# First feed-forward of a decoder trunk: the fifth quad's weight forms join the written-out order, and squares, norm, gates and first down chunk come later

## The chip, the core and the metric

The kernel runs as one program on one core of a Trainium2 chip. The metric is the device time of one execution in microseconds (us); smaller is better. A core has several engines that work side by side, each through a queue of its own that is taken strictly in the order in which the program lists it: PE (matrix products), DVE (elementwise), ACT (elementwise with tables, copies), POOL, and SP, which here only issues transfers. An instruction waits for other engines by semaphores, and what stands behind it on its engine waits with it.

## The reference

A trunk of two layers on a sequence of 512 positions and width 1024. Each layer adds half of a gated feed-forward, a mixer with three head groups, and half of a second feed-forward. What is touched here is the very first feed-forward:

```
def _rmsnorm(x, g):
    y = xf * lax.rsqrt(jnp.mean(xf * xf, axis=-1, keepdims=True) + EPS)
    return (y * g.astype(jnp.float32)).astype(x.dtype)

def _swiglu(x, w_gate, w_up, w_down):
    return (jax.nn.silu(x @ w_gate) * (x @ w_up)) @ w_down

x = x + MACARON * _swiglu(_rmsnorm(x, ffn1_norm), ffn1_w_gate, ffn1_w_up, ffn1_w_down)
```

The width of the hidden layer is 2816; all is float32.

## The kernel before

Activations lie transposed: 1024 features in four pairs of 128-row blocks (`x0` to `x3`), 512 positions along a row. Each float32 operand of a product is split into a high part (a rounded copy that ACT makes, L89) and a low part (the difference, which DVE makes, L90); one product is then three matmuls, high by high, high by low, low by high. Function `parts` (L87) issues the two halves of such a split.

The columns of the gate and up weights are taken in 22 quads of 256 columns by 512 positions, gates and ups in turn. A quad isn't multiplied in the plain way but by seven products of half size (a Strassen-like scheme), each of 12 matmuls of 128 rows by 256 columns. Products 1, 2 and 3 use three weight blocks directly (tile `wd`), products 6 and 7 use sums of blocks (tile `wa`), products 4 and 5 others (tile `wb`). Function `forms_steps` (L132) gives the steps that build them: `direct` makes `wd`, `first` adds two blocks (L148) and makes `wa`, `second` adds two (L154) and makes `wb`. Tiles `wa` and `wb` come from one pool tag with three buffers (`w2`). The result of a product is fetched from the accumulator by ACT or DVE in `after` (L349 to L366): product 1 is copied by L353, 2 added by L355, 6 copied by L357, 5 by L359, 7 subtracted at L361, 3 at L363, 4 copied by L365. Products 1, 6, 7 and 4 of a quad share one accumulator (`pa`), so PE can't start product 6 before ACT has copied product 1 away.

The norm isn't applied to `x` ahead of the products. Products take the raw `x` with its gain, and the reciprocal root of the mean square is multiplied in when a gate is finished. So the squares (L237 on ACT, the sums L240 and L243 on DVE), the column sums (`norm_columns`: four small matmuls L250, then L252 and a power on POOL, L254) and the row form (`norm_rows`: L264, four matmuls L265, copy L267) may come late, but before the first `done` (L368), which multiplies a gate by that row, applies Silu on ACT, multiplies again, and later multiplies the up half by the gate and splits the result into tile `h`.

The first two quads are multiplied in the plain way in function `start` (L419), while `x` and weights arrive. There, within `tc.manual_schedule`, the instructions of DVE and ACT stand in the order in which the code lists them; everything else is ordered by the scheduler from priorities and buffer counts. Quads 2 and 3 have their forms in the set order; quad 4 (whose weights lie in separate tiles, `rawa`) has its own made later, by `begin` (L329). A list of products, in `gate_up` (L308), says when each product and each block of the down projection (`schedule`, L502) is to come; function `start` returns a list of calls made after the products, one each: the tenth is `norm_columns`, the twelfth `norm_rows` with the two first `done`. The tag `u` has two buffers, which the up results and the tiles of squares share.

Of the kernel before, what the change touches and what calls it, by code (L numbers as in the profile page):

```python
# [9 lines left out]
F32 = mybir.dt.float32  # L10
F32R = mybir.dt.float32r
AF = mybir.ActivationFunctionType
ALU = mybir.AluOpType
AX = mybir.AxisListType

P = 128
D = 1024
T = 512
# [9 lines left out]
KP = KT // 2  # L28
# [20 lines left out]
def trunk(ctx, tc, xt, w_first, w_gu1, w_dn1, w_in, w_out, w_gu2, w_dn2, w_last, par, con, wst, bst, gvr, gain, out):  # L49
    nc = tc.nc  # L50
# [2 lines left out]
    wpool = ctx.enter_context(tc.tile_pool(name="wpool", bufs=1))  # L53
    spool = ctx.enter_context(tc.tile_pool(name="spool", bufs=2))
    pp = ctx.enter_context(tc.tile_pool(name="pp", bufs=8, space=bass.MemoryType.PSUM))
    stage = {}

    def bank(name):
        return pp.tile([P, T], F32, tag="ps", name=name)
# [6 lines left out]
    def uniq(s):  # L66
        uid[0] += 1
        return f"{s}{uid[0]}"
# [18 lines left out]
    def parts(hi, lo, src):  # L87

        nc.scalar.copy(hi, src)  # L89
        nc.vector.tensor_tensor(lo, src, hi.bitcast(F32), ALU.subtract)  # L90

    def load(src):
        n = src.shape[-1] * (src.shape[1] if len(src.shape) == 3 else 1)
# [79 lines left out]
    split = parts  # L173


    state = {}
    warm_ps = bank("warm")
    xf = [None] * KP

# [55 lines left out]
    def squares(m):  # L235
        sq = scratch(1, "sq")
        nc.scalar.activation(sq, xp[m], AF.Square)  # L237
        if m == 0:
            state["acc"] = spool.tile([P, T], F32, tag="acc", name=uniq("acc"), bufs=1)
            nc.vector.tensor_tensor(state["acc"], sq[:, :T], sq[:, T:], ALU.add)  # L240
        else:
            for i in range(2):
                nc.vector.tensor_tensor(state["acc"], state["acc"], sq[:, i * T : (i + 1) * T], ALU.add)  # L243
# [64 lines left out]
    def gate_up(w_gu, first, others, tail, from_start=False):  # L308
# [7 lines left out]
        quads = [(p, j) for p in range(FP) for j in range(2)]  # L316
        steps = [(7 * q + t, 0, q, n) for q in range(len(quads)) for n, t in WHEN.items()]
        if from_start:
            moved = {(3, 1): 15.3, (3, 2): 15.6, (2, 4): 27.5}
            steps = [(moved.get((q, n), t), k, q, n) for t, k, q, n in steps]  # L320
        steps += [(t, 1, None, work) for t, work in others]
        steps.sort(key=lambda e: e[:2])
        live, gates, raws = {}, {}, {}
# [25 lines left out]
        def after(q, n):  # L349
            c11, c21, c12, c22 = [quarter(q, i) for i in range(4)]  # L350
            b = live[q]
            if n == 1:
                state["copied"] = nc.scalar.copy(c11, b["pa"])  # L353
            elif n == 2:
                nc.vector.tensor_tensor(c11, b["pb"], c11, ALU.add)  # L355
            elif n == 6:
                state["copied"] = nc.scalar.copy(c12, b["pa"])  # L357
            elif n == 5:
                state["copied"] = nc.scalar.copy(c22, b["pc"])  # L359
            elif n == 7:  # L360
                nc.vector.tensor_tensor(c22, c22, b["pa"], ALU.subtract)  # L361
            elif n == 3:
                nc.vector.tensor_tensor(c12, b["pc"], c12, ALU.subtract)  # L363
            else:
                nc.scalar.copy(c21, b["pa"])  # L365
                done(q)  # L366

        def done(q):  # L368
            p, j = quads[q]
# [18 lines left out]
        else:  # L388
            begin(0)
            begin(1)  # L390
            for m in range(KP):
                for q in (0, 1):
                    for n in (1, 2):
                        ps = psum(q, ("pa", "pb")[n - 1])
                        hi, lo = live[q]["w"][n]
                        bh, bl = form(m, MOVING[n])
                        c = slice(m * P, (m + 1) * P)
# [4 lines left out]
            wait = lambda: None  # L402
# [16 lines left out]
    def start(live, done, ahead, raws_of):  # L419

        for k in range(12):
            warm = warm_ps[:, (k % 4) * P : (k % 4 + 1) * P]
            nc.tensor.matmul(warm, lhsT=ones, rhs=ones, start=True, stop=True)
        pool = stage["pool"]
        extra = pool.tile([P, 4 * T], F32R, tag="hp", name="a21", bufs=4)
        a21 = [(extra[:, m * H : (m + 1) * H], extra[:, (4 + m) * H : (5 + m) * H]) for m in range(KP)]
        raws = [wpool.tile([P, 1024], F32, tag="pt", name=uniq("rawp"), bufs=3) for _ in range(KP - 1)]  # L430
        raws.append(wpool.tile([P, 12 * P], F32, tag="wdn", name=uniq("rawp"), bufs=2)[:, :1024])
        for k in (1, 0):
            nc.sync.dma_start(x[k], xt[:, k, :])
            nc.sync.dma_start(raws[0][:, (1 - k) * T : (2 - k) * T], w_first[0, :, (1 - k) * T : (2 - k) * T])
        for m in range(1, KP):
            nc.sync.dma_start(xp[m], xt[:, 2 * m : 2 * m + 2, :])
            nc.sync.dma_start(raws[m], w_first[m])
        ahead(2)
        ahead(3)
        ahead(4)  # L440
        ws, rooms = [], []
        steps2 = forms_steps(raws_of(2))
        steps3 = None
        with tc.manual_schedule(engines={mybir.EngineType.DVE, mybir.EngineType.Activation}):
            for m in range(KP):
                w = wpool.tile([P, 2048], F32R, tag="w2", name=uniq("wf"), bufs=3)
                ws.append(w)
                if m == 0:
                    parts(w[:, :T], w[:, 1024 : 1024 + T], raws[m][:, :T])
                norm_pair(m, G1, True)  # L450
                gained(m, 0, G1, a21[m][0], a21[m][1], slice(H, T))
                if m == 0:
                    parts(w[:, T:1024], w[:, 1024 + T :], raws[m][:, T:])
                else:
                    parts(w[:, :1024], w[:, 1024:], raws[m])
            for m in range(KP):
                r = pool.tile([P, 4 * T], F32, tag="hp", name=uniq("xw"), bufs=4)
                rooms.append(r)
                sums_of(m, G1, r[:, : 4 * H], r[:, 4 * H : 6 * H])
                if m:  # L460
                    sum_parts(m - 1, rooms[m - 1][:, : 4 * H])
                if m == 1:
                    steps2[1]()
            steps3 = forms_steps(raws_of(3))
            steps3[1]()
            sum_parts(KP - 1, rooms[KP - 1][:, : 4 * H])
            for f in steps2[2:] + steps3[2:]:
                f()
        ahead(5)
        ps = [[bank(uniq("pg")) for _ in range(2)] for _ in range(2)]  # L470
        for m in range(KP):
            kw = {"skip_group_check": True}
            for j in range(2):
                b11, b21, b22, b12 = [
                    [ws[m][:, o + j * T + i * P : o + j * T + (i + 1) * P] for o in (0, 1024)] for i in range(4)
                ]
                hi, lo = xf[m][:, H : 3 * H], xf[m][:, 8 * H : 10 * H]
                for i, w in ((0, b21), (1, b22)):
                    mm3(ps[j][i], w[0], w[1], hi, lo, m == 0, False, **kw)
                for i, w in ((0, b11), (1, b12)):  # L480
                    for t, a in ((slice(0, H), form(m, A11)), (slice(H, T), a21[m])):
                        mm3(ps[j][i][:, t], w[0], w[1], a[0], a[1], False, m == KP - 1, **kw)
        for j in range(2):
            c = pool.tile([P, 2 * T], F32, tag="gu"[j], name=uniq("gu"[j]), bufs=2)
            for i in range(2):
                nc.scalar.copy(c[:, i * T : (i + 1) * T], ps[j][i])
            live[j] = {"c": c}
        for j, w in ((0, steps2[0]), (1, steps3[0])):
            c = pool.tile([P, 2 * T], F32, tag="gu"[j], name=uniq("gu"[j]), bufs=2)
            live[2 + j] = {"w": w, "c": c}  # L490
        for m in range(KP):
            squares(m)

        def rows():
            norm_rows()
            done(0)
            done(1)

        wait = lambda: None
        return [wait] * 9 + [norm_columns, wait, rows]  # L500

    def schedule(l, w_dn, hs):  # L502

        def run(d, p0, p1):
            p = bank(uniq("pdn"))
            block_down(p, l, w_dn, d, 2 * p0, hs[2 * p0 : 2 * p1], True, True)
            add_down(d, p)

        held = {}

        def fetch_first(d):
            with tc.issue_after(state["fetched"].ins):
                held[d] = down_raw(l, w_dn, d, 0, 2 * CHUNKS[0][1])

        def split_first(d):
            with tc.issue_after(state["copied"].ins):
                held[d] = down_parts(held[d], 2 * CHUNKS[0][1])

        def run_first(d):
            p = bank(uniq("pdn"))  # L520
            down_products(p, held.pop(d), hs[: 2 * CHUNKS[0][1]], True, True)
            add_down(d, p)

        jobs = []
        for p0, p1 in CHUNKS[:-1]:
            for d in range(KT):
                t = 14 * p1 + 10 + 3.5 * d
                if p0:
                    jobs.append((t, lambda d=d, p0=p0, p1=p1: run(d, p0, p1)))
                else:  # L530
                    jobs.append((t - 10, lambda d=d: fetch_first(d)))
                    jobs.append((t - 4, lambda d=d: split_first(d)))
                    jobs.append((t, lambda d=d: run_first(d)))
        return jobs

    def ffn(l, w_gu, w_dn, after):
        with tc.tile_pool(name=uniq("ffn"), bufs=1, reuse_waits="tile") as pool:
# [6 lines left out]
                opened[d] = bank(uniq("pdn"))  # L544
                block_down(opened[d], l, w_dn, d, f0, hs[f0:f1], True, False)

            others = schedule(l, w_dn, hs)
            others += [(14 * p1 + t, lambda d=d: open_block(d)) for d, t in enumerate((0, 3, 6, 7))]

            def tail():  # L550
# [407 lines left out]
```

## Time and profile before

| what | us |
|---|---|
| three timed runs | 1816.51, 1817.70, 1818.04 |
| their median | 1817.7 |
| the profiled execution, whole time | 1817.61 |
| its span, first to last instruction | 1815.9 |
| PE busy in the span | 1802.4 (99%) |
| DVE busy | 1326.5 (73%) |
| ACT busy | 826.1 (45%) |
| POOL busy | 121.0 (7%) |

The span is what the trace covers; 1.7 us of the profiled execution lie around it. A busy PE isn't a PE at its peak: matmuls are pipelined, so the distance from start to start counts, not the length of a row. In rows of the timeline the first number is the start, the second the duration; a bracket at the end gives the idle time before the instruction and what ended it.

### The profile page before, as it was taken

How to read it: one execution, taken by the hardware profiler on the slowest of the kernel's cores; microseconds unless marked ns; L12 is line 12 of the kernel's file. 1: busy time of each engine (PE TensorE's matmuls, PEld its weight loads, DVE VectorE, ACT ScalarE, POOL GpSimd, SP SyncE). 2: the span in 40 equal slices, each digit the busy share in tenths (PEclk: the TensorE clock that was granted, in tenths of full speed). 3: DMA queues.
4: the chain of work that ended last, by engine and by line, in shares of the span. 5: the costliest groups of instructions: out<-in, count | busy, mean ns of one | idle time of the engine just before them, and what ended most of it. 6: DMA issues, size and time to landing. Idle time of an engine off the chain costs nothing.

```text
span 1815.9 us, 28447 instructions
## 1 busy us (share of the span) xinstructions
PE 1802.4 (99%) x11576; PEld 1646.1 (91%) x11576; DVE 1326.5 (73%) x1828; ACT 826.1 (45%) x1224; POOL 121.0 (7%) x121
## 2 busy tenths in 40 slices
PE   9999999999999999999999999999999999999998
PEld 8999999888889999999899999998888899999996
DVE  8877777674687877777888777766657788777765
ACT  7544444413345544444554444434133455444443
POOL 1100000000100000000000000000000000000000
PEclk9999999999999999999999999999999999999999
DMA  7665655522223855556457555573322257565632
GB/s 244 164 160 153 153 145 150 176 81 93 70 82 82 223 145 151 150 156 157 128 129 197 148 152 148 152 190 115 98 70 70 70 144 196 151 155 157 157 88 82
DMA packets 120899, 251.19 MB, mean 138 GB/s; under 512 B 10048, under 2 KB 12352, under 8 KB 120512
## 3 DMA queue, kind: packets, MB, share of 16 engines
q1 hardware_dynamic: 97072, 204.02, 35.5%
q0 software_dynamic: 23408, 45.09, 15.3%
q8 instruction: 90, 1.47, 0.3%
q14 instruction: 41, 0.34, 0.1%
q10 hardware_dynamic: 288, 0.27, 0.0%
HBM read 247.25 MB, written 2.10 MB: 137 GB/s over the span
## 4 chain that ended last, share of the span: by engine, by line
PE 94%; DVE 4%; issue 1%; ACT 1%; DMA 0%; POOL 0%; SPq 0%; POOLq 0%; ACTq 0%; DVEq 0%
PE pa L281 9%; PE pa L282 9%; PE pa L283 9%; PE pdn L169 8%; PE pdn L170 8%; PE pdn L171 8%; PE pc L282 4%; PE pc L283 4%; PE pc L281 4%; PE pb L283 2%; PE pb L282 2%; PE pb L281 2%; PE pqk L169 2%; PE pqk L171 2%; PE pqk L170 2%; PE pout L171 2%
## 5 line engine op out<-in xcount | busy, mean ns | idle before, releaser
L169 PE MATMUL pdn<-h,wdn 128*128 128x512 f32 x632 | 247.6, 392 | 0.0
L170 PE MATMUL pdn<-h,wdn 128*128 128x512 f32 x632 | 247.6, 392 | 0.0
L171 PE MATMUL pdn<-h,wdn 128*128 128x512 f32 x632 | 246.0, 389 | 0.3 <-DVE wdn L90 0.3
L89 ACT CAST wd<-rawq 128x1024 fp32r<-128x1024 f32 (+1 forms) x170 | 133.4, 832 | 183.8 <-PE pc L283 170.3
L281 PE MATMUL pa<-xf,wa 128*128 128x256 f32 x688 | 195.7, 284 | 1.5 <-ACT g L353 1.5
L283 PE MATMUL pa<-xf,wa 128*128 128x256 f32 x688 | 195.3, 284 | 0.2 <-DVE wa L90 0.2
L282 PE MATMUL pa<-xf,wa 128*128 128x256 f32 x688 | 195.2, 284 | 0.0
L90 DVE TENSOR_TENSOR wd<-rawq,wd 128x1024 fp32r<-128x1024 f32 (+1 forms) x170 | 155.3, 954 | 48.6 <-ACT wd L89 48.4
L89 ACT CAST wdn<-rawd 128x512 fp32r<-128x512 f32 (+1 forms) x152 | 97.2, 639 | 176.2 <-PE pdn L171 173.5
L112 POOL DMA_DIRECT2D rawq<-in_w_gu x85 | 93.0, 1095 | 1241.7 <-DMA rawq<-in_w_gu 806.1
L89 ACT CAST w<-raw 128x1024 fp32r<-128x1024 f32 x77 | 80.9, 1051 | 205.3 <-PE pqk L171 60.6
L90 DVE TENSOR_TENSOR w<-raw,w 128x1024 fp32r<-128x1024 f32 x77 | 94.1, 1222 | 70.5 <-ACT w L89 69.8
L171 PEld LDWEIGHTS pdn<-h,wdn 128*128 128x128 f32 x632 | 118.7, 188 | 26.4 <-DVE wdn L90 0.7
L169 PEld LDWEIGHTS pdn<-h,wdn 128*128 128x128 f32 x632 | 119.2, 189 | 21.0
L170 PEld LDWEIGHTS pdn<-h,wdn 128*128 128x128 f32 x632 | 119.2, 189 | 19.5
L281 PEld LDWEIGHTS pa<-xf,wa 128*128 128x128 f32 x688 | 132.5, 193 | 2.6 <-ACT g L353 1.7
L283 PEld LDWEIGHTS pa<-xf,wa 128*128 128x128 f32 x688 | 132.6, 193 | 0.5 <-DVE wa L90 0.4
L90 DVE TENSOR_TENSOR wdn<-rawd,wdn 128x512 fp32r<-128x512 f32 (+1 forms) x152 | 107.0, 704 | 35.4 <-ACT wdn L89 35.4
L282 PEld LDWEIGHTS pa<-xf,wa 128*128 128x128 f32 x688 | 132.6, 193 | 0.0
L306 DVE SCALAR_TENSOR_TENSOR x<-pdn,x 128x512 f32<-128x512 f32 x152 | 103.8, 683 | 3.8 <-PE pdn L171 3.8
L90 DVE TENSOR_TENSOR wa<-rawq,wa 128x1024 fp32r<-128x1024 f32 x85 | 103.6, 1219 | 1.9 <-ACT wa L89 1.9
L90 DVE TENSOR_TENSOR wb<-rawq,wb 128x1024 fp32r<-128x1024 f32 x85 | 103.5, 1218 | 0.2 <-ACT wb L89 0.2
(283 smaller groups left out, 5041.1 us busy)
## 6 DMA issues: line engine op xcount, KB each, us to landing
rawq<-in_w_gu SPq DMA_DIRECT2D x170, 512.0 KB, 5.7
rawq<-in_w_gu POOLq DMA_DIRECT2D x85, 512.0 KB, 5.8
rawd<-in_w_dn SPq DMA_DIRECT2D x140, 256.0 KB, 4.5
raw<-in_w_in SPq DMA_DIRECT2D x52, 512.0 KB, 3.5
rawq<-in_w_gu SPq DMA_DIRECT2D x85, 256.0 KB, 6.0
raw<-in_w_out SPq DMA_DIRECT2D x16, 512.0 KB, 3.5
rawd<-in_w_dn SPq DMA_DIRECT2D x12, 384.0 KB, 3.2
raw<-in_w_last SPq DMA_DIRECT2D x6, 512.0 KB, 4.1
```

What stands on the lines that cost most here:

```text
L89: nc.scalar.copy(hi, src)
L90: nc.vector.tensor_tensor(lo, src, hi.bitcast(F32), ALU.subtract)
L112: nc.gpsimd.dma_start(two[:, :, 1, :], src.rearrange("p (n s c) -> p n s c", n=2, s=2)[:, :, 0, :], accum_op=ALU.add)
L169: nc.tensor.matmul(ps, lhsT=ah, rhs=bh, start=first, stop=False, **kw)
L170: nc.tensor.matmul(ps, lhsT=ah, rhs=bl, start=False, stop=False, **kw)
L171: nc.tensor.matmul(ps, lhsT=al, rhs=bh, start=False, stop=last, **kw)
L281: nc.tensor.matmul(ps, lhsT=hi[:, c], rhs=bh, start=one, stop=False, skip_group_check=True)
L282: nc.tensor.matmul(ps, lhsT=hi[:, c], rhs=bl, start=False, stop=False, skip_group_check=True)
L283: nc.tensor.matmul(ps, lhsT=lo[:, c], rhs=bh, start=False, stop=m == pairs[-1], skip_group_check=True)
L306: nc.vector.scalar_tensor_tensor(x[d], p, 0.5, x[d], ALU.mult, ALU.add)
```

## The change

Five edits, all but one within the first feed-forward's start.

- The forms of quad 4 (`steps4`) are built at the end of the set order, after those of quads 2 and 3, not by `begin`.
- The squares of the four pairs are issued behind the last low-part difference that was recorded (`state["split"]`).
- The norm's columns come after the sixteenth product of the list, its rows after the eighteenth, not the tenth and twelfth.
- The four first gates and ups aren't finished as their products end or two at once, but one after each of the next four products (`gates`). The results of the first two quads lie in one tile of tag `hp`.
- Product 4 of quad 2 isn't moved in the list any more, and the first chunk of the down projection is due 7 steps later.

```diff
@@ gate_up @@
-            moved = {(3, 1): 15.3, (3, 2): 15.6, (2, 4): 27.5}
+            moved = {(3, 1): 15.3, (3, 2): 15.6}
@@ after @@
                 nc.scalar.copy(c21, b["pa"])
-                done(q)
+                if not (from_start and q < 4):
+                    done(q)
@@ start @@
-            for f in steps2[2:] + steps3[2:]:
+            steps4 = forms_steps(raws_of(4))
+            for f in steps2[2:] + steps3[2:] + steps4[1:]:
                 f()
...
-            c = pool.tile([P, 2 * T], F32, tag="gu"[j], name=uniq("gu"[j]), bufs=2)
+            if j == 0:
+                c01 = pool.tile([P, 4 * T], F32, tag="hp", name=uniq("c"), bufs=4)
+            c = c01[:, 2 * j * T : 2 * (j + 1) * T]
...
-        for j, w in ((0, steps2[0]), (1, steps3[0])):
+        for q, w in ((2, steps2[0]), (3, steps3[0]), (4, steps4[0])):
...
-        for m in range(KP):
-            squares(m)
-        def rows():
-            norm_rows()
-            done(0)
-            done(1)
+        with tc.issue_after(state["split"].ins):
+            for m in range(KP):
+                squares(m)
         wait = lambda: None
-        return [wait] * 9 + [norm_columns, wait, rows]
+        gates = [lambda q=q: done(q) for q in range(4)]
+        return [wait] * 15 + [norm_columns, wait, norm_rows] + gates
@@ schedule @@
-                t = 14 * p1 + 10 + 3.5 * d
+                t = 14 * p1 + 10 + 3.5 * d + (0 if p0 else late)
```

What this makes of the engines' queues is seen in three places. Lines of the changed kernel are one lower than those of the kernel before.

ACT at the very start of the program, while `x` arrives; before:

```order
L201 ACTIVATE a_105<-x_70,pcol 128x256
L89 CAST wf_142<-rawp_106 128x512
L201 ACTIVATE xf_155<-x_71,pcol 128x512
L201 ACTIVATE xf_155<-x_71,pcol 128x256
L201 ACTIVATE a_105<-x_71,pcol 128x256
L89 CAST wf_154<-rawp_107 128x1024
L201 ACTIVATE xf_165<-x_72,pcol 128x512
```

And in the changed kernel:

```order
L200 ACTIVATE a_105<-x_70,pcol 128x256
L89 CAST wf_142<-rawp_106 128x512
L236 ACTIVATE sq_419<-x_70 128x1024
L200 ACTIVATE xf_155<-x_71,pcol 128x512
L200 ACTIVATE xf_155<-x_71,pcol 128x256
L200 ACTIVATE a_105<-x_71,pcol 128x256
L89 CAST wf_154<-rawp_107 128x1024
L236 ACTIVATE sq_423<-x_71 128x1024
```

Two of the four squares now stand among the first splits of `x`, each ahead of the next pair's.

ACT where quads 3 and 4 begin (`u` belongs to quad 3, `wa_250`, `wb_254` and `g_418` to quad 4, `sq` are squares), in the changed kernel, with the semaphores that each waits for:

```order
L89 CAST wa_250<-rawa_131 128x1024 [waits DMASW3_49,DVE_49,Activation_49]
L352 COPY g_418<-pa_597 128x256 [waits PE_49]
L356 COPY g_418<-pa_597 128x256 [waits PE_49]
L89 CAST wb_254<-rawa_130 128x1024 [waits DVE_49,DMASW2_49,PE_49,Activation_49]
L236 ACTIVATE sq_427<-x_72 128x1024 [waits DVE_49]
L236 ACTIVATE sq_431<-x_73 128x1024 [waits DVE_49]
L352 COPY u_417<-pa_463 128x256 [waits DVE_49,Activation_49]
```

Before, the copy of quad 3's first product stood among the direct forms of quad 4 and ahead of all its `wa` and `wb`:

```order
L237 ACTIVATE sq_416<-x_73 128x1024 [waits DVE_49,Activation_49]
L89 CAST wd_614<-rawa_132 128x512 [waits DMAHW3_49,PE_49]
L89 CAST wb_239<-rawq_125 128x1024 [waits DVE_49]
L89 CAST wd_614<-rawa_130 128x512 [waits DMAHW4_49]
L353 COPY u_403<-pa_448 128x256 [waits DVE_49,Activation_49]
L89 CAST wd_614<-rawa_131 128x512 [waits DMAHW5_49]
```

So the copy of `pa_463` moved behind quad 4's last split and the last two squares. The wait of `wb_254` for PE is for its buffer: the semaphore's value is that of the last matmul that reads `wa_250`. The wait of `u_417` is for the tile of `sq_427`, whose buffer it takes.

DVE in the same place, in the changed kernel:

```order
L90 TENSOR_TENSOR wb_254<-rawa_130,wb_254 128x1024 [waits Activation_49]
L239 TENSOR_TENSOR acc_421<-sq_419 128x512
L242 TENSOR_TENSOR acc_421<-acc_421,sq_423 128x512 [waits DVE_49] x2
L242 TENSOR_TENSOR acc_421<-acc_421,sq_427 128x512 [waits DVE_49,Activation_49]
L242 TENSOR_TENSOR acc_421<-acc_421,sq_427 128x512 [waits DVE_49]
L242 TENSOR_TENSOR acc_421<-acc_421,sq_431 128x512 [waits DVE_49,Activation_49]
```

All seven sums of squares stand in one run behind `wb_254`; before, they stood in between the splits and sums of quads 2 and 3. On PE the 24 matmuls of `pa_597<-wa_250` (products 6 and 7 of quad 4) are followed by those of `pa_463<-wa_235` (product 6 of quad 3), the first of which waits for the copy `u_417`. From the 921st matmul on, PE's list is the same in both kernels.

## Rows read from the trace of the kernel before

**Rows 1.** Busy time and instructions of PE, PEld, DVE, ACT, POOL; then PEclk, DMA.
```profile
12.00:35.00 23.00, 23.00 (x160) 21.30 (x160) 22.54 (x37) 18.70 (x28) 4.10 (x4) 1.00 0.95 276
35.00:50.00 15.00, 13.37 (x91) 12.36 (x91) 13.79 (x24) 8.78 (x13) 2.49 (x2) 0.89 0.54 139
50.00:65.00 15.00, 13.48 (x112) 13.09 (x111) 13.70 (x16) 10.83 (x16) 1.14 (x1) 1.00 0.61 160
65.00:80.00 15.00, 15.00 (x109) 14.15 (x108) 14.46 (x21) 9.86 (x14) 1.09 (x1) 1.00 0.42 134
80.00:95.00 15.00, 15.00 (x108) 14.10 (x107) 11.33 (x16) 6.40 (x12) 1.09 (x1) 1.00 0.88 200
```

**Rows 2.** Timeline of PE: start, duration, instruction, idle time before it.
```profile
36.06 0.38 PE L283 MATMUL pa<-xf,wa 128*128 128x256 f32 x1 [0.25 <-DVE wa L90]
...
37.75 0.39 PE L281 MATMUL pc<-xf,wb 128*128 128x256 f32 x1 [0.24 <-ACT wb L89]
...
42.43 0.28 PE L282 MATMUL pc<-xf,wd 128*128 128x256 f32 x1
42.55 0.28 PE L283 MATMUL pc<-xf,wd 128*128 128x256 f32 x1
43.72 0.39 PE L281 MATMUL pa<-xf,wb 128*128 128x256 f32 x1 [0.90 <-DVE g L361]
...
46.34 0.41 PE L281 MATMUL pa<-xf,wa 128*128 128x256 f32 x1
46.56 0.41 PE L282 MATMUL pa<-xf,wa 128*128 128x256 f32 x1
...
52.23 1.05 PE L265 MATMUL psr<-dg,ones 128*128 128x128 f32 x8
...
62.47 0.39 PE L281 MATMUL pa<-xf,wa 128*128 128x256 f32 x1 [1.52 <-ACT g L353]
```

**Rows 3.** Granted clock (third number from the end) in three stretches, columns as in Rows 1.
```profile
46.00:49.40 3.40, 3.40 (x18) 3.40 (x18) 2.46 (x10) 0.26 (x1) 1.41 (x1) 0.50 0.97 164
...
1808.00:1812.00 4.00, 0.00 (x0) 0.00 (x0) 2.78 (x6) 2.11 (x5) 0.54 (x1) 0.84 0.34 131
1812.00:1816.00 4.00, 0.00 (x0) 0.00 (x0) 0.00 (x0) 0.00 (x0) 0.00 (x0) 0.50 0.34 133
```

**Rows 4.** Timeline of ACT at the start and in the first quads.
```profile
9.30 1.12 ACT L201 ACTIVATE xf<-x,pcol 128x512 fp32r<-128x512 f32 x2 [0.76 <-DMA x<-in_xt]
...
10.73 1.04 ACT L89 CAST wf<-rawp 128x1024 fp32r<-128x1024 f32 x1
11.90 1.12 ACT L201 ACTIVATE xf<-x,pcol 128x512 fp32r<-128x512 f32 x2
...
34.66 1.06 ACT L237 ACTIVATE sq<-x 128x1024 f32<-128x1024 f32 x1
...
44.86 0.36 ACT L353 COPY u<-pa 128x256 f32<-128x256 f32 x1
...
55.15 1.28 ACT L375 ACT_TABLE_LOAD   x1
56.44 2.01 ACT L375 ACTIVATE g<-g 128x1024 f32<-128x1024 f32 x2
```

**Rows 5.** Timeline of DVE in the first quads.
```profile
32.98 0.68 DVE L148 TENSOR_TENSOR rawq<-rawq 128x512 f32<-128x512 f32 x1
33.59 0.69 DVE L240 TENSOR_TENSOR acc<-sq 128x512 f32<-128x512 f32 x1
...
36.53 1.41 DVE L243 TENSOR_TENSOR acc<-acc,sq 128x512 f32<-128x512 f32 x2
...
43.26 0.41 DVE L361 TENSOR_TENSOR g<-g,pa 128x256 f32<-128x256 f32 x1
43.59 0.68 DVE L243 TENSOR_TENSOR acc<-acc,sq 128x512 f32<-128x512 f32 x1
...
54.18 2.35 DVE L374 TENSOR_TENSOR g<-g,rr 128x1024 f32<-128x1024 f32 x2
```

More of the change, by code (lines that the diff above doesn't have):

```diff
@@ L55, in trunk @@
     pp = ctx.enter_context(tc.tile_pool(name="pp", bufs=8, space=bass.MemoryType.PSUM))
-    stage = {}
+    stage, state = {}, {}
     def bank(name):
@@ L89, in parts @@
         nc.scalar.copy(hi, src)
-        nc.vector.tensor_tensor(lo, src, hi.bitcast(F32), ALU.subtract)
+        state["split"] = nc.vector.tensor_tensor(lo, src, hi.bitcast(F32), ALU.subtract)
     def load(src):
@@ L173, in trunk @@
     split = parts
-    state = {}
     warm_ps = bank("warm")
@@ L487, in start, with schedule @@
             live[j] = {"c": c}
-        for j, w in ((0, steps2[0]), (1, steps3[0])):
+        for q, w in ((2, steps2[0]), (3, steps3[0]), (4, steps4[0])):
+            j = q % 2
             c = pool.tile([P, 2 * T], F32, tag="gu"[j], name=uniq("gu"[j]), bufs=2)
-            live[2 + j] = {"w": w, "c": c}
-        for m in range(KP):
-            squares(m)
-        def rows():
-            norm_rows()
-            done(0)
-            done(1)
+            live[q] = {"w": w, "c": c}
+        with tc.issue_after(state["split"].ins):
+            for m in range(KP):
+                squares(m)
         wait = lambda: None
-        return [wait] * 9 + [norm_columns, wait, rows]
-    def schedule(l, w_dn, hs):
+        gates = [lambda q=q: done(q) for q in range(4)]
+        return [wait] * 15 + [norm_columns, wait, norm_rows] + gates
+    def schedule(l, w_dn, hs, late=0):
         def run(d, p0, p1):
@@ L545, in open_block @@
                 block_down(opened[d], l, w_dn, d, f0, hs[f0:f1], True, False)
-            others = schedule(l, w_dn, hs)
+            others = schedule(l, w_dn, hs, 7 if l == 0 and w_gu is w_gu1 else 0)
             others += [(14 * p1 + t, lambda d=d: open_block(d)) for d, t in enumerate((0, 3, 6, 7))]
```

## The prediction, as put on record before the changed kernel ran

> **What bounds the kernel now.** I read the busy time by engine first: PE is busy in 99% of the span, so a change can pay only where PE stands idle or runs at its lower clock, and it costs wherever it makes PE wait. Next the stretches of the first 95 us [rows 1]. From 12 to 35 us PE is full and DVE almost so (22.54 of 23.00). From 35 to 65 us PE loses 1.63 and 1.52 us while DVE is still busy for 13.8 of 15: quads 2 to 4 begin there. From 65 us on PE is full again; DVE has some 0.5 us to spare until 80 us and 3.7 us from 80 to 95 us. Then the timeline of PE [rows 2]: its idle times are small ones (0.25, 0.24), one of 0.90 us behind DVE and one of 1.52 us behind an ACT copy. Two matmuls of 256 columns start 0.12 us apart when nothing holds them (42.43, 42.55). The one behind the 0.90 us wait started 1.17 us after the one ahead of it (42.55 to 43.72) instead of 0.12, so a wait of 0.90 costs 1.05: its idle time and some 0.15 us of restart. Last the clock [rows 3]: from 46.0 to 49.4 us it was granted at 0.50 (1.2 of 2.4 GHz); two matmuls there start 0.22 us apart (46.34, 46.56), so of these 3.40 us about 1.5 (0.10 of every 0.22) are lost.
>
> All that the change can win is therefore what PE loses here: 3.15 us of idle time, about 0.7 us of restarts, 1.5 us of clock. What it may lose isn't bounded that way.
>
> **The change part by part.** Durations: an ACT pass over 128x1024 takes 1.04 to 1.06, a copy of 256 columns 0.36, the table load 1.28 and two Silus 2.01 [rows 4]. On DVE 512 columns take 0.68 (starts 0.61 apart), two of them 1.41, 256 columns 0.41 (0.33 from start to start), and 1024 columns half of 2.35, about 1.17 [rows 5].
>
> *Squares at the start of ACT.* Before, no square stood there; the first shown takes 1.06 at 34.66. Now sq_419 stands where ACT had been idle 0.76 us for `x` (9.30), and sq_423 stands ahead of the split of the third pair, which started at 11.90 [rows 4]. Bounds: 0, if later idle time of ACT and DVE takes it up, and 0.3 + 1.06 = 1.35 us if nothing does. DVE, which takes ACT's output, has only 0.46 us idle from 12 to 35 us [rows 1], so I take 0.85: the forms of quad 2 come 0.85 us later, and the wait at 36.06 grows from 0.25 to about 1.0.
>
> *Sums of squares out of the forms.* The seven sums (0.69 and 1.41 for a pair, in rows 5) no longer stand among the splits of quads 2 and 3. DVE gains 7 x 0.61 = 4.3 us up to quad 4's end, so what PE waits for at 43.72 (the subtraction at 43.26, which queued among them) comes no later than before, while PE arrives 0.85 later: the wait of 0.90 takes up the delay and shrinks to 0.1 to 0.4. Of the small waits after it I count 0.4 as gone. Both edits together: +0.85 - 0.85 - 0.4 = -0.4. Bounds: -1.5 (the delay is swallowed ahead and the waits go) and +0.9 (the waits stay).
>
> *Quad 4's forms in the set order.* PE now runs the products 6 and 7 of quad 4 (`pa_597<-wa_250`) back to back and early. Before, the trace shows no such pair. Two new waits: the third matmul needs the low half of wa_250, which DVE makes behind ACT's cast (1.17 by 1024 columns, less what PE does meanwhile), and product 7 can't start before ACT has copied product 6 from the same accumulator (copy 0.36 and two hand-offs). Nearest row for a wait behind an ACT copy is 1.52, for one behind DVE 0.90 [rows 2]; bounds 0.3 and 2.4. I take 0.7 + 0.5 and 0.3 for two restarts: +1.5.
>
> *The chain behind it.* This is the largest term. wb_254 takes the buffer of wa_250, so ACT can't cast it before PE has ended those 24 matmuls. Everything of ACT and DVE that follows is behind that cast: first DVE's split of wb_254, then the sums, which stand behind it in a run, and only then the copy u_417, because its tile is the one that sq_427 leaves when the sums have read it. PE's next matmul, `pa_463`, waits for u_417. All of it is in series with PE: cast 1.04, split 1.17, first sum 0.69, sq_423's two 1.41, sq_427's two 1.41, copy 0.36 = 6.1, and three or four hand-offs between engines, about 0.1 each: 6.4, and 0.1 for the restart: +6.5. Before, the copy of quad 3's first product stood at 44.86 with nothing of quad 4's `wa` or `wb` ahead [rows 4]. Bounds: 5.5 (starts 0.61 apart instead of whole durations, no hand-off) and 7.0.
>
> *Norm and gates later.* The column and row products keep their matmuls; only their place moves. The first Silu, with its table load, now stands ahead of u_715, the copy of quad 5's first product, on ACT. From the end of the four `dg` on DVE: split of wd_716 1.17, a 0.33 subtraction, 0.68 and L148's 0.68; then ACT's casts wa_722 and wb_726 (2.08), table load 1.28, one Silu 1.00, copy 0.36: 7.6 us. PE has the row form (1.05, at 52.23 in rows 2) and 36 matmuls of 0.12: 5.4. A wait of about 2.2 us, which takes the place of the 1.52 at 62.47 [rows 2]: +0.6. Bounds: -1.5 (covered) and +1.5 (no overlap at all).
>
> In the trace the table load starts at 55.15 and the Silu at 56.44, right behind its 1.28 us [rows 4]. The Trainium skill, *ScalarE: Activation LUTs*, "What ACT_TABLE_LOAD costs", adds a drain of some 1380 ns to a load of 1283 ns. By it this term would be 1.4 us longer and the time 1829.8; the trace shows the load and no drain, so it has no part in the sum.
>
> *DVE in arrears.* While PE stands in the long wait DVE does only the sums; its gate multiplications (L374, L376, L379), which before began at 54.18 [rows 5], now come behind the row form, after that wait. When PE starts quad 5's products again, DVE has until the split of the first down weights (wdn_846) eight passes of 1024 columns, three of 256 and one of 512: 8 x 1.14 + 3 x 0.33 + 0.7 = 10.8 us (1.14 being starts within a run, 1.17 less 0.03). PE has 76 matmuls and some restarts, 76 x 0.12 + 0.5 = 9.6. That leaves 0.9 to 1.2; the next two waits are of the same kind and size (the `wa` and `wb` of quad 6 behind L148 and L154), 0.86 and 0.62 by the same count. With restarts +2.6. Against it speaks that DVE had 3.7 us to spare from 80 to 95 us [rows 1], which is why the arrears end there; if all of that comes in time the term is 0, and with no overlap it is 3.5.
>
> *At nothing.* The first down chunk seven steps later: the same blocks in another place, on a full PE. The weights of quads 5 and 6 are fetched later but, by the DMA share of 0.42 from 65 to 80 us [rows 1], have room, and are used some 20 us after they are asked for. If that cover fails, it costs one transfer's delay, below 2 us. The `hp` tile changes no instruction. From the 921st matmul on PE's list is the same.
>
> Sum at full clock: -0.4 + 1.5 + 6.5 + 0.6 + 2.6 = +10.8.
>
> *The clock.* The half-clock stretch followed a thin time of PE (13.37 busy of 15, rows 1). In the changed kernel PE is fuller just before, so this stretch may go (-1.5), but it stands still for 6.4 us later. At the end of the program, where PE has ended, the clock goes to 0.84 and then 0.50 within 8 us [rows 3], so I expect PE to start again at 0.50 and to lose between 1.5 (a stretch like that at 46.0) and 3.0 us (twice as long). I take 1.5 gone and 1.5 new: 0.
>
> In the trace it fell at 46.0 us with no pause over 0.90 us ahead, and did not fall behind the 1.52 us wait, the stretch from 50 to 65 us being at 1.00 [rows 1 to 3]. The Trainium skill, *TensorE: Matmul & The Clock Gate*, "Why this matters for your kernels", holds that pauses between bursts put TensorE back to its lower clock. By it alone the long wait costs clock, as I have it; by the row a thin stretch does too, which is rival B.
>
> Against its own execution of 1817.61 (span 1815.9 and 1.7 around it) that gives 1817.6 + 10.8 = 1828.4. The execution lies 0.1 below the median of the runs, so nothing is to be shifted.
>
> **The rivals.**
> A, the forecast: 1828.4, within 1826.5 and 1830.5.
> B, the clock falls twice, after the 6.4 us wait and again behind the 2.2 us one or between the three waits near 86 to 92 us. For it: the fall at 46.0 after a mere thinness [rows 2, 3]. Against: none after 1.52 us. Each is worth 1.5 to 3: about 1831.5.
> C, DVE and ACT use the long wait of PE to catch up, so the arrears (2.6) and the 0.6 vanish: 1817.6 + 10.8 - 3.2, about 1825.3. For it: 3.7 us of spare time [rows 1]. Against: the queue order leaves DVE little but sums to do in it.
> D, not slower: DVE is the true bound of this part. It is busy for 41.95 of the 45 us from 35 to 80 us [rows 1], its list is the same work in another order, and so a wait of PE would only be paid back in the waits that follow, the 3.15 us of idle time being gained and half of it kept: about 1816. It decides if DVE stands idle for less than 3 us between 50 and 72 us; by the chain it waits some 10 us there, behind ACT's cast and for PE.
> E, the order of the queues doesn't bring the waits that I read off, since PE reaches these points later than I think: the 6.5 halves and the rest stays, 1825.
>
> **How the numbers follow.** A 0.65, B 0.13, C with E 0.14, D 0.08. A measurement of this kernel can tell 0.2%, 3.6 us, from no change: A, B, C and E lie over 1821.3, where D lies below 1817.7. A few parts of C and E could come under 1821.3 if two terms fall together: slower 0.92; of D half would lie under 1814.1, with the clock's 1.5 gained too: faster 0.04, and the other half same. The range takes in C (1825.3) with the low ends of the chain (-1.0) and of the waits at quad 4 (-1.2), 1823, and B, 1831.5, with little above it: 1823 to 1832.
>
> **What would show it.** ACT has a square near 8.5 and one near 11.8 us; PE's wait at about 36 us is 1.0 and that at 43.7 us at most 0.4. PE stands idle for about 6.4 us, ending near 60 us with a matmul `pa<-xf,wa` released by the ACT copy of L352 into `u`, with DVE's five sums in the time before; the clock is 0.50 behind that. A second idle time of about 2.1 us near 75 us has the table load ahead of its copy; three of 0.6 to 0.9 us follow between 85 and 93 us, and past 100 us both kernels run at the same distance. I am wrong if the copy of u comes ahead of the sums, if PE's longest pause is below 4 us, or if what is lost up to 95 us comes back later.

## The result: 11 us slower, as forecast

| | us |
|---|---|
| kernel before, four runs | 1816.51 to 1818.04, median 1817.83 |
| changed kernel, four runs | 1828.42 to 1829.37, median 1828.91 |
| ratio, with its 95% interval | 1.0062 [1.0045, 1.0080] |
| profiled execution of the changed kernel, span | 1827.2 (before 1815.9) |

The forecast was 1828.4. Run again beside two of the experiments on another chip, the changed kernel took 1829.15, a ratio of 1.0064 [1.0051, 1.0077].

The same stretches as in [rows 1], from the trace of the changed kernel; columns are the stretch, its length, busy time and instructions of PE, PEld, DVE, ACT and POOL, the granted clock, the DMA share and GB/s:

```profile
12.00:35.00 23.00, 22.68 (x157) 20.80 (x156) 22.10 (x35) 17.65 (x27) 4.10 (x4) 1.00 0.95 274
35.00:50.00 15.00, 13.74 (x104) 12.64 (x103) 10.37 (x14) 7.55 (x12) 1.08 (x1) 1.00 0.44 123
50.00:65.00 15.00, 7.58 (x43) 6.97 (x43) 7.89 (x12) 4.55 (x7) 1.08 (x1) 0.77 0.61 158
65.00:80.00 15.00, 13.42 (x113) 13.21 (x112) 11.20 (x18) 9.40 (x14) 1.05 (x1) 1.00 0.10 23
80.00:95.00 15.00, 13.23 (x94) 11.90 (x93) 14.67 (x19) 9.65 (x14) 1.14 (x1) 1.00 0.53 135
```

Before, PE lost 1.63 and 1.52 us from 35 to 65 us and nothing after. Now it loses 1.26, then 7.42, then 1.58 and 1.77. DVE, which had 13.79 and 13.70 us of work from 35 to 65 us, has 10.37 and 7.89: from 50 to 65 us it idles for half the time. That row alone says that DVE isn't the bound there; PE, ACT and DVE wait for each other in turn.

The waits of PE from 30 to 100 us, the same trace; after the releaser come the sum, the number of waits and the longest:

```profile
PE pa L280 <- ACT u L352: 8.1, 2, 6.5
PE pa L282 <- DVE wa L90: 1.2, 2, 0.8
PE pa L280 <- ACT wa L89: 0.7, 1, 0.7
PE pdn L171 <- DVE wdn L90: 0.7, 1, 0.7
PE pc L280 <- ACT wb L89: 0.7, 2, 0.4
PE pa L280 <- ACT g L356: 0.5, 1, 0.5
PE pa L280 <- DVE g L360: 0.2, 1, 0.2
```

One of them is most of the loss. PE's timeline around the waits that answer to [rows 2]:

```profile
36.97 0.39 PE L282 MATMUL pa<-xf,wa 128*128 128x256 f32 x1 [0.76 <-DVE wa L90]
...
43.79 0.39 PE L280 MATMUL pa<-xf,wb 128*128 128x256 f32 x1 [0.17 <-DVE g L360]
...
50.79 0.39 PE L282 MATMUL pa<-xf,wa 128*128 128x256 f32 x1 [0.48 <-DVE wa L90]
...
52.70 0.39 PE L280 MATMUL pa<-xf,wa 128*128 128x256 f32 x1 [0.46 <-ACT g L356]
54.12 0.28 PE L282 MATMUL pa<-xf,wa 128*128 128x256 f32 x1
60.87 0.58 PE L280 MATMUL pa<-xf,wa 128*128 128x256 f32 x1 [6.47 <-ACT u L352]
61.25 0.41 PE L281 MATMUL pa<-xf,wa 128*128 128x256 f32 x1
61.47 0.42 PE L282 MATMUL pa<-xf,wa 128*128 128x256 f32 x1
...
77.82 0.39 PE L280 MATMUL pa<-xf,wa 128*128 128x256 f32 x1 [1.58 <-ACT u L352]
...
88.37 0.50 PE L171 MATMUL pdn<-h,wdn 128*128 128x512 f32 x1 [0.73 <-DVE wdn L90]
```

From 54.12 to 60.87 no matmul starts. What fills that time stands on ACT and DVE, one behind the other. ACT:

```profile
54.48 1.04 ACT L89 CAST wb<-rawa 128x1024 fp32r<-128x1024 f32 x1 [1.83 <-PE pa L282]
57.42 1.06 ACT L236 ACTIVATE sq<-x 128x1024 f32<-128x1024 f32 x1 [1.89 <-DVE acc L239]
58.87 1.06 ACT L236 ACTIVATE sq<-x 128x1024 f32<-128x1024 f32 x1 [0.39 <-DVE acc L242]
60.45 0.37 ACT L352 COPY u<-pa 128x256 f32<-128x256 f32 x1 [0.52 <-DVE acc L242]
```

And DVE:

```profile
55.56 1.22 DVE L90 TENSOR_TENSOR wb<-rawa,wb 128x1024 fp32r<-128x1024 f32 x1 [3.88 <-ACT wb L89]
56.70 0.68 DVE L239 TENSOR_TENSOR acc<-sq 128x512 f32<-128x512 f32 x1
57.42 3.74 DVE L242 TENSOR_TENSOR acc<-acc,sq 128x512 f32<-128x512 f32 x5
```

Read from the top: PE's last matmul of `pa<-wa` releases ACT's cast at 54.48; its end releases DVE's split at 55.56; the sums run from 56.70; the copy at 60.45 starts when the first four of the five grouped sums are done; PE starts 0.42 us later. The copy itself takes 0.37 us, and it waits for no matmul: its tile alone holds it back.

The clock, 2 us at a time (granted clock third from the end):

```profile
56.00:58.00 2.00, 0.00 (x0) 0.00 (x0) 1.97 (x3) 0.58 (x1) 0.00 (x0) 1.00 1.15 212
58.00:60.00 2.00, 0.00 (x0) 0.00 (x0) 1.83 (x4) 1.53 (x2) 0.00 (x0) 0.56 0.11 17
60.00:62.00 2.00, 1.13 (x5) 1.13 (x6) 1.90 (x4) 0.65 (x2) 0.00 (x0) 0.50 0.04 8
62.00:64.00 2.00, 2.00 (x11) 2.00 (x11) 0.09 (x1) 0.16 (x1) 0.00 (x0) 0.50 0.00 0
64.00:66.00 2.00, 2.00 (x15) 2.00 (x14) 0.00 (x0) 0.21 (x1) 0.00 (x0) 0.73 0.00 0
66.00:68.00 2.00, 2.00 (x20) 2.00 (x18) 0.85 (x2) 0.69 (x1) 0.00 (x0) 1.00 0.00 0
```

It falls to 0.50 (1.2 GHz) within the pause and is back at 1.00 in the row from 66 us on. From 60.87 to 65.08 the matmuls start 0.21 to 0.22 us apart (61.25, 61.47), the first step alone being 0.38: 19 steps in 4.21 us, where 0.12 each makes 2.28, so 1.9 us are lost, 0.26 of it in the restart. The stretch at 0.50 that the kernel before had from 46.0 us [rows 3] is gone: 46.0 to 49.4 us now has 1.00. It may not come in every execution of the kernel before: of its 55 timed runs beside the experiments, the 13 with a mean granted clock of 0.999 took 1815.94 to 1816.88 us, and no slower one has that clock; the traced one, with the fall, had 0.998 and took 1817.61 us. Only one is traced, so this isn't shown.

### The profile page after: what moved, and what is told of

Same layout as the page of the kernel before. It is cut to its first block, busy times and chain, and to the rows that moved or that the text cites. A ratio compares the mean times of both kernels' runs of the same rounds, so it can differ in the third digit from the quotient of the medians.

```text
span 1827.2 us, 28453 instructions
## 1 busy us (share of the span) xinstructions
PE 1805.2 (99%) x11576; PEld 1647.9 (90%) x11576; DVE 1327.9 (73%) x1828; ACT 825.2 (45%) x1224; POOL 120.6 (7%) x121
## 4 chain that ended last, share of the span: by engine, by line
PE 93%; DVE 4%; ACT 1%; issue 1%; DMA 0%; POOL 0%; SPq 0%; POOLq 0%; ACTq 0%; DVEq 0%
PE pa L280 9%; PE pa L282 9%; PE pa L281 9%; PE pdn L169 8%; PE pdn L170 8%; PE pdn L171 8%; PE pc L281 4%; PE pc L282 4%; PE pc L280 4%; PE pb L282 2%; PE pb L281 2%; PE pb L280 2%; PE pqk L169 2%; PE pqk L171 2%; PE pout L171 2%; PE pqk L170 2%
```

## The experiments

The theory is the prediction's: the pause of 6.5 us is one series of cast, split, sums and copy, and each link counts in full. Its rivals are that DVE has too much work in any order, so that what is saved comes back later, and that a single one of the edits makes the loss whatever the others do. Each run was compared with the kernel before on its own chip (there 1816.9 to 1817.6); ratios have their 95% interval, and the changed kernel's is 1.0062.

**Two more sums in the series (sums_more).**

```
-                nc.vector.tensor_tensor(state["acc"], state["acc"], sq[:, i * T : (i + 1) * T], ALU.add)
+                for _ in range(2 if m == 2 and "rr" not in state else 1):
+                    nc.vector.tensor_tensor(state["acc"], state["acc"], sq[:, i * T : (i + 1) * T], ALU.add)
```

> The changed kernel with the two sums of the third pair's squares (sq_427) done twice each, two more passes of 512 columns on DVE between wb_254's split and the copy u_417; the mean square is then too large, nothing else changes. Theory (all of the long wait of PE is one series: cast, split, sums, copy): the pause of 6.5 us grows by two passes, 2 x 0.61 to 0.72 = 1.2 to 1.4 us, to about 7.8, and the time by the same, 1830.2. Rival (DVE has slack there, the pause is set by ACT's cast behind PE and by the buffers): the pause stays at 6.5 and the time at 1828.9.

Measured 1830.34, 1.0073 [1.0058, 1.0088]; span 1828.7, 1.5 longer. PE's longest wait in its trace:

```profile
PE pa L281 <- ACT u L353: 7.9, 1, 7.9
```

7.9 for 6.5: the two passes appear in full (DVE's group of five takes 3.74 us in the changed kernel, that of seven 5.19 here, 1.45 more), and the waits behind it stay as they were, so nothing later gives them back. That the span grew by just as much is in part chance: the half clock behind the pause cost 2.4 us here for 1.9, while the changed kernel's wait at 13.27 us (0.5 with its restart) didn't come. The sums are links of the series, as the theory has it.

**Quad 4's last form, taken out of the set order (wb4_scheduled).** The edit takes its cast on ACT and its split on DVE out together.

```
-            for f in steps2[2:] + steps3[2:] + steps4[1:]:
+            for f in steps2[2:] + steps3[2:] + steps4[1:3]:
 ...
                 squares(m)
+        steps4[3]()
```

> The changed kernel, but only the last form of quad 4 (wb_254) is taken out of the set order and left to the scheduler. Theory: ACT's copy of quad 3's first product then no longer stands behind a cast that waits for PE's last reader of wa_250; the pause of 6.5 us shrinks to some 1.5 to 2 us (the sums still stand there), and with no long standstill the clock stays at 1.00, 1.7 us more: 1828.9 - 4.7 - 1.7, about 1822.5 to 1824. Rival (DVE is in arrears and the work only moves): the pauses near 77, 88 and 94 us grow by what is saved and the time stays above 1827. Rival (the clock falls behind a wait of 1.5 as well): 1824.2.

Measured 1822.47, 1.0031 [1.0017, 1.0044]; span 1820.3. PE's timeline where the pause was:

```profile
53.80 0.28 PE L282 MATMUL pa<-xf,wa 128*128 128x256 f32 x1
55.53 0.39 PE L280 MATMUL pa<-xf,wa 128*128 128x256 f32 x1 [1.45 <-ACT u L352]
55.75 0.28 PE L281 MATMUL pa<-xf,wa 128*128 128x256 f32 x1
```

ACT's timeline in the same place:

```profile
52.68 1.06 ACT L236 ACTIVATE sq<-x 128x1024 f32<-128x1024 f32 x1 [0.34 <-DVE acc L242]
54.16 1.04 ACT L89 CAST wb<-rawa 128x1024 fp32r<-128x1024 f32 x1 [0.42 <-PE pa L282]
55.11 0.37 ACT L352 COPY u<-pa 128x256 f32<-128x256 f32 x1
```

The busy time of the stretch from 54 to 58 us, with the granted clock third from the end:

```profile
54.00:58.00 4.00, 2.55 (x19) 2.29 (x19) 3.02 (x5) 1.96 (x4) 0.00 (x0) 1.00 1.09 274
```

The step across the wait is 1.73 us instead of 6.75: 5.0 us. Matmuls start 0.22 and then 0.12 apart behind it, so the 1.9 us of clock are saved too: 6.9, and the span is 6.9 shorter (the medians, from two chips, differ by 6.4). The waits behind it stay as they were (1.6, 0.7, 0.7, 0.4), so nothing comes back, and the place of one form in the queues of ACT and DVE makes 6.9 of the 11.3 us. ACT's queue shows what is different: the two squares now run at 51.02 and 52.68, while PE is still at work, and so do most of the sums on DVE. The expectation had the size right for a wrong reason: the copy still stands behind the cast that waits for PE. Cast and copy, 1.04 and 0.37, with their hand-offs make the 1.45 us that are left; what has gone from the series is the split, the sums and the squares.

**The squares' tie (squares_scheduled).**

```
-        with tc.issue_after(state["split"].ins):
-            for m in range(KP):
-                squares(m)
+        for m in range(KP):
+            squares(m)
```

> The changed kernel, with the squares again issued without a tie to the last split, so the scheduler places them; the four other edits stay. Theory (the squares' tie makes the series behind wb_254): no pause of 6 us is left, ACT copies quad 3's first product long before; some 2 us are lost near 35 us since squares and sums then stand ahead of quad 2's forms; the time is within 2 us of the kernel before, 1816 to 1820. Rival (quad 4's forms in the set order are what costs, the squares only stand by): a pause of 4 us or more stays between 50 and 62 us and the time is above 1824.

Measured 1817.97, 1.0006 [0.9996, 1.0015]: no difference from the kernel before, with the four other edits in place. No wait of PE from 35 to 65 us is over 0.8 us, and DVE is busy for 11.46 of the 15 us from 50 to 65. A cost of the squares is left at 34 us, where a step of PE grows by 1.41 us: the last of the four squares now begins on ACT at 19.15 us, so that all stand ahead of quad 2's forms. So the pause of 6.5 us needs both, the tie and the place of quad 4's last form; without the tie nothing of it is left, without that place 1.45 us.

**Quad 4 out of the set order (q4_by_begin)**, `steps4` removed and its quad made by `begin` as before.

> The changed kernel, but quad 4's forms are again made by begin, outside the set order; squares stay tied to the last split, which is now quad 3's. Theory: the squares' run then stands behind quad 3's forms, whose copy doesn't wait for a buffer of quad 4, so the pause of 6.5 us becomes one of about 1.6 near 51 us; the waits near 78 to 85 us stay: about +2 to +3 against the kernel before, 1819 to 1821. Rival (the tie of the squares alone makes the loss): a pause of 4 us or more stays and the time is above 1824.

Measured 1820.35, 1.0015 [1.0006, 1.0025]. The longest wait in place of the pause is 1.4 us, for ACT's cast of quad 4's `wa`. Together with the run before: the tie alone costs 1.4 us at that place, the set order alone nothing there, both 6.5.

**The gates two products later (gates_later).**

```
-        return [wait] * 15 + [norm_columns, wait, norm_rows] + gates
+        return [wait] * 15 + [norm_columns, wait, norm_rows, wait, wait] + gates
```

> The changed kernel, with the four gates two products later (after the twenty-first to the twenty-fourth). Theory of arrears: u_715 is copied ahead of the table load, so the wait of 1.6 us near 77 us goes, but the same ACT and DVE work is then late near 87 us, where a wait of 2 us or so takes its place; within 1 us of the changed kernel, 1828 to 1829. Rival (the wait near 77 us is a loss of its own): the time falls by 1.7 us or more, below 1827.5.

Measured 1829.33, 1.0065 [1.0051, 1.0079]. PE's waits from 70 to 100 us:

```profile
PE pa L280 <- DVE u L360: 2.2, 1, 2.2
PE pc L280 <- ACT wb L89: 0.7, 1, 0.7
PE pa L282 <- DVE wd L90: 0.3, 1, 0.3
```

The 1.6 us behind the table load is gone and 2.2 us behind a subtraction of DVE has come: 3.2 in all, 3.5 in the changed kernel. By this run these waits are arrears, which move. The time didn't fall by that 0.3 us; the half clock behind the pause cost 2.6 us in this trace for 1.9.

**The place of the first chunk (chunk_early, chunk_early_beside).**

```
-            others = schedule(l, w_dn, hs, 7 if l == 0 and w_gu is w_gu1 else 0)
+            others = schedule(l, w_dn, hs, 0)
```

> The changed kernel, with the first chunk of the down projection due where it was before (no 7 steps later). Theory: the long pause and the clock stay; only the waits behind it change: DVE's arrears from 85 to 95 us (0.73, 0.7, 0.4 us) are met by other work, so the time falls by 0.5 to 2 us, 1827 to 1828.4. Rival (the chunk was put later because DVE and ACT can't make its splits in time): the waits behind 75 us grow and the time goes over 1829.5.

> The changed kernel once more, beside the next one, so that the place of the first chunk can be weighed on one chip. Both theories: 1.0062 of the kernel before, as measured, some 1828 to 1829.

> The changed kernel with the first chunk at its old place, beside the changed kernel on one chip. Theory (the later chunk leaves PE without other work while DVE is in arrears from 78 to 95 us): 0.8 to 1.8 us less than the changed kernel. Rival (the place of the chunk is worth nothing, as the prediction had it; the first comparison was two chips): within 0.5 us of it.

The first run gave 1827.18, 1.0055 [1.0040, 1.0070]; the pair on one chip 1826.90 (five runs, 1826.54 to 1827.30) against 1829.15 (1828.59 to 1829.56). The runs of the two don't overlap: 2.25 us, somewhat more than expected. PE's waits from 70 to 100 us with the chunk at its old place (chunk_early_beside):

```profile
PE pa L280 <- ACT u L356: 0.6, 1, 0.6
PE pdn L169 <- ACT h L89: 0.3, 1, 0.3
PE pdn L170 <- DVE h L90: 0.2, 1, 0.2
PE pa L282 <- DVE wa L90: 0.2, 1, 0.2
```

1.2 us (from the unrounded waits) for 3.5. The arrears of DVE and ACT are the same work; PE has the chunk's blocks to run meanwhile.

**Squares after products of the list (squares_in_list, squares_in_list_chunk3).**

```
-        with tc.issue_after(state["split"].ins):
-            for m in range(KP):
-                squares(m)
+        for k, f in zip([6, 8, 10, 12], [lambda m=m: squares(m) for m in range(KP)]):
+            at.setdefault(k, []).append(f)
```

`at` maps a place in the list of products to what is called there, norm and gates too, which stay where they were; the second kernel has the chunk 3 steps later in place of 7.

> The changed kernel, with each pair's squares called after the seventh, ninth, eleventh and thirteenth product of the list instead of being tied to the last split. Theory: ACT has no square in the start (the wait of 0.32 at 13.3 us goes), none ahead of quads 2 and 3's forms, and the sums fill DVE's time between 45 and 60 us; what is left is about 0.9 near 36, 0.5 near 69 and the three of 0.6 to 0.9 from 75 to 82 us; faster than the kernel before by 1 to 3.5 us, 1813.5 to 1816. Rival (the sums come too late for the norm's columns, and PE waits there for them): over 1819.

Measured 1816.45, 0.9995 [0.9986, 1.0005]: half a microsecond over the expected range, and no difference from the kernel before.

> The changed kernel with the squares called after the seventh to thirteenth product, as in an earlier run here, and the first chunk 3 steps later than in the kernel before, not 7. Theory (the waits of 0.4 to 0.9 us from 70 to 83 us are the chunk's: PE has no other block to take while DVE makes up its arrears): most of the 2.9 us that these waits cost there go, one of about 0.4 us stays near 72 us; 1813.5 to 1815. Rival (they are DVE's alone and move with it): they come back elsewhere before 100 us and the time stays at 1816 to 1817.

Measured 1814.65, 0.9984 [0.9975, 0.9993], faster than the kernel before. PE's waits from 60 to 100 us in the first of the two:

```profile
PE pa L280 <- ACT wa L89: 0.7, 1, 0.7
PE pa L280 <- ACT u L356: 0.7, 1, 0.7
PE pc L280 <- ACT wb L89: 0.4, 1, 0.4
PE pdn L171 <- DVE wdn L90: 0.4, 1, 0.4
```

And in the second:

```profile
PE pdn L170 <- DVE h L90: 0.3, 1, 0.3
PE pdn L171 <- DVE wdn L90: 0.2, 1, 0.2
```

2.3 us against 0.4 (both unrounded). These waits are there without any long pause ahead: those for the `wa` and `wb` casts have the size that they have in the changed kernel (0.73 and 0.45 for 0.73 and 0.44), so they aren't its consequence; the one for `wdn` is 0.43 for 0.73, so a part of that one can be. The chunk's place removes them.

**A version from the parts (best_of_parts)**: quad 4 by `begin`, squares at places 8, 10, 12 and 13, norm at 16 and 18, gates at 19 to 22, chunk 3 steps later.

> From the changed kernel: quad 4's forms made by begin, squares called after the ninth, eleventh, thirteenth and fourteenth product, norm after the seventeenth and nineteenth, gates after the next four, first chunk 3 steps later. Theory: between 36 and 80 us only waits of 0.9, 0.4 and 0.3 us are left of what PE lost, and the clock doesn't fall: 3.4 us of waits and 1.5 of clock less than the kernel before, 1812.5 to 1815. Rival (DVE's work up to 95 us is too much in any order, so it comes back behind 80 us): 1816.5 to 1819.

Measured 1813.97 (1813.57 to 1814.58), 0.9982 [0.9973, 0.9991]: faster than both kernels. From 35 to 110 us PE waits three times:

```profile
PE pa L282 <- DVE wa L90: 0.8, 1, 0.8
PE pdn L170 <- DVE h L90: 0.3, 1, 0.3
PE pc L280 <- ACT wb L89: 0.2, 1, 0.2
```

DVE is as busy as before (14.05 and 13.58 us from 35 to 65), and the clock from 46.0 to 49.4 us is 1.00. Quad 2's product 4, no longer moved, and the `hp` tile stand in all these kernels, so what they are worth by themselves is not shown.

## Why the prediction was right, and where it was not

Steps are distances from start to start, less 0.12 us.

| term | forecast | measured |
|---|---|---|
| squares at the start, sums out of the forms | -0.4 | -0.3 |
| quad 4's two waits | +1.5 | 0.64 + 0.62 = +1.3 |
| the chain | +6.5 | 6.75 - 0.12 = +6.6 |
| gates behind the table load, against before's 1.68 | +0.6 | 1.74 - 1.68 = +0.1 |
| arrears, 88 to 95 us | +2.6 | 0.89 + 0.89 + 0.60 = +2.4 |
| clock | 0 | 1.9 - 1.5 = +0.4 |
| sum | +10.8 | +10.5 of 11.3 |

0.8 us of the difference of the spans isn't in the table. The wait at 13.27 us (a step of 0.71 for 0.23) is a part of it, and some 0.2 lie near 143 us, where a down block starts; the rest is in steps too small to separate. Two sums of the prediction are rounded down: 2.2 less 1.52 is 0.7 and not 0.6, and 0.9 to 1.2 with 0.86, 0.62 and three restarts of 0.15 is 2.8 to 3.1 and not 2.6.

**The chain** stands row by row as it was counted: the cast ends up behind PE, the split behind the cast, the sums behind the split, the copy behind the sums. The added sums show that a link counts in full; wb4_scheduled shows that squares and sums run under PE's work once the cast and the split no longer stand ahead of them. The sizes were a little off both ways: the hand-offs, put at 0.1 each without a row, are 0.04 to 0.08 (54.48 and 1.04 to 55.56, 60.45 and 0.37 to 60.87), and the sums up to the copy took some 3.7 us for the 3.5 counted. Rival E, a pause of half the length, is out.

**The squares at the start** stand at 8.48 and 11.86 us on ACT, DVE's first sum for quad 2's forms (L148) begins at 33.89 for 32.98 [rows 5], 0.91 later where 0.85 was forecast, and the wait at 36.97 us is 0.76 for the 0.25 of [rows 2]; at 43.79 us 0.17 is left of 0.90. A wait of 0.8 near 36.9 us stands in squares_in_list too, for another reason: no square is at the start there, but the cast of quad 2's `wa` (34.52) stands behind a copy of `u` that waits for PE (34.25). A new wait of 0.32 us at 13.27 us, for the first weights, is in this trace; it is also in that of squares_in_list (0.52), which has no square at the start, and not in that of sums_more, which has; so it isn't the squares'.

**The gates** came out smaller. The chain from the end of `dg` took about the time that was counted (70.3 to 77.8 us, 7.5 for 7.6), but PE's row form began half a microsecond behind the end of `dg`, at 70.88, and so PE came to the copy later: a wait of 1.58, not 2.2. In the trace the table load starts at 75.16 and Silu at 76.45, again 1.29 later, so the 1380 ns of drain that the Trainium skill, *ScalarE: Activation LUTs*, "What ACT_TABLE_LOAD costs", adds are not in this kernel either.

**The first chunk** is the step that was mis-sized: costed at nothing, it is worth 2.2 us. The sum came out all the same, by luck: the waits of this order were counted under the gates and the arrears, so that two errors met. The explanation beside them was wrong in the main. They aren't what DVE missed during the long pause: squares_in_list has no pause, and most of these waits. They are DVE's and ACT's load from 65 to 95 us with no block of the chunk for PE to run in between. Rival C expected them to vanish when DVE catches up in the pause; they didn't, and DVE idled in it, as was argued against it.

**The clock**: one fall, as in the forecast, in the pause and not after 1.6 us or later, against rival B; its price was 1.9 for 1.5. The rule of the Trainium skill, *TensorE: Matmul & The Clock Gate*, "Why this matters for your kernels", that long pauses between bursts put TensorE back to its lower clock, agrees with the pause of 6.47 us, behind which the clock is 0.50. Behind the pause of 1.45 us in wb4_scheduled it stayed at 1.00, though PE was busy there for only 2.55 of 4.00 us: a thin stretch alone, on which the prediction and rival B leaned, did not bring a fall. The fall of the kernel before at 46.0 us, with no pause over 0.90 ahead, is in none of the other twelve traces; what made it stays open, and so does how much of the forecast gain of 1.5 us there was to win in each run.

**Rival D** is out: DVE idled for 7.1 us from 50 to 65 us, and the waits of PE were not paid back.

## What to carry to other kernels

When work is written into a fixed order on a queue, look for the instruction in it that waits for an engine further down the chain, and for what stands behind it: here a cast that waited for PE's last reader of a buffer stood ahead of squares and sums, and these ahead of the copy on which PE's next product waited. Put ahead of the cast, the same squares and sums ran under PE's work. Work that can come at any time is best given a place in the list after which it has room, as in squares_in_list, not tied to the end of the order, where it becomes a link. And a block that PE can run at any time is worth what it covers: cost its move by the waits that were under it.

## What was not expected of the hardware

Behind the pause in which the clock fell, the restart is slower too: the second matmul started 0.38 us after the first (60.87, 61.25) and the following ones 0.21 to 0.22 apart, where behind the wait of 1.45 us at full clock it was 0.22 (55.53, 55.75) and then 0.12. In the changed kernel the matmuls behind the pause ran at 0.50 for 4.2 us, which cost 1.9 us beyond the pause itself. This price isn't the same in every execution: behind a pause of the same length it was 1.9 us in the second trace of the changed kernel, 2.4 in chunk_early_beside, 2.6 in gates_later and 2.8 in chunk_early, where the clock came back only 6.2 us after the restart. Two traces with the same pause can so differ by 0.9 us, more than some of the waits that are compared here.
